# MLA's rotated queries with both terms on 128 rows, and low parts and sums of squares moved from GpSimd to VectorE

## The chip, the cores and the metric

The kernel runs on one core of a Trainium2 chip. TensorE does the matrix products and writes them into PSUM; VectorE, ScalarE and GpSimd do the elementwise work; SyncE (SP) issues most of the DMA transfers. The metric is the time on the device of one execution in microseconds (us), lower is better.

## The reference

The reference is a two-layer transformer block on 512 tokens of width 1024, in float32. Each layer has a mixer with four branches, and a gated feed-forward part; both are followed by a normalised residual sum. The branch that matters here is MLA, attention from latents, with 4 heads of 64 plain and 32 rotated dimensions:

```python
    q = heads(rms_norm(cq, mla_q_norm) @ w_uq, MLA_HEADS)
    kv = heads(rms_norm(ckv, mla_kv_norm) @ w_ukv, MLA_HEADS)
    k_rope = jnp.broadcast_to(rope(kr[:, None], pos), (B, MLA_HEADS, S, MLA_ROPE))
    q_mla = jnp.concatenate([q[..., :MLA_NOPE], rope(q[..., MLA_NOPE:], pos)], axis=-1)
    k_mla = jnp.concatenate([kv[..., :MLA_NOPE], k_rope], axis=-1)
    o_d = causal_block_attention(q_mla, k_mla, kv[..., MLA_NOPE:], (MLA_NOPE + MLA_ROPE) ** -0.5)
...
    x = x + rms_norm(mix, g_post_mix[l])
    h = rms_norm(x, g_pre_ffn[l])
    f = (jax.nn.silu(h @ w_ffn_gate[l]) * (h @ w_ffn_up[l])) @ w_ffn_down[l]
    x = x + rms_norm(f, g_post_ffn[l])
```

Rotation multiplies each rotated pair by a cosine and a sine and adds the two terms. `rms_norm` needs the sum of the squares of 1024 values for each token.

## The kernel before

All values lie transposed, features on the 128 partitions and the 512 tokens along the row. To reach float32 accuracy, every factor of a product is split into a high part (a rounded copy, made by ScalarE) and a low part (value minus high part, made by VectorE or GpSimd), and each product is made of three matmuls. `split_to` does this for activations (L483 high, L484 low; L486 and L487 with a scale). `conversion` does it for weights that a DMA brought (L297 high, L298 low).

The layer runs in this order: latents (a product with the weights of all branches' inputs), the four branches interleaved with each other, `out_block` (gates merged, output product, residual sum), the feed-forward part, and in layer 0 `down_block`, which already starts the latents of layer 1. `mla_prepare` is a generator that is advanced step by step between the other branches' products; work put off with `defer` runs one step later. It transposes the normalised latents, rotates the shared key (columns 128 to 192 of `ck`), transposes it (L867) to PSUM rows 64 to 96, and copies it to the keys of all four heads (`shared`). For each head it makes the query product (128 rows: 64 plain, 32 for the cosine and 32 for the sine term, arranged by the weights), and `q_out` scales, rotates and splits it to 96 rows. The values go through `v_split` (L928 to L933, half a PSUM bank each). Then the heads' scores (L634) are made, query block by query block, each by three matmuls; VectorE adds the mask and takes the row's maximum (L643), ScalarE takes the exponential (L645, with a load of its function table at the first), VectorE the reciprocal (L652), GpSimd scales (L653), and TensorE transposes the result (L660).

`square_sums` squares the eight column blocks of the new x on ScalarE (L1296) and adds four of them on GpSimd and four on VectorE (L1297), then both sums (L1035); TensorE sums over the partitions (L532, `token_sums`), and `rms_steps` and `root` make the factor: 1/sqrt with one correction (L516 to L524). `spread` (L562) brings the factor to all partitions by a matmul.

In `down_block` the new x, its normalised form and its high and low parts come by a generator (`renewal`, L1306 to L1312), half of the tokens at a time, while the latents' products of layer 1 (`latent_steps`, L1005 to L1007: high weight by high value, low weight by high value, high weight by low value) run in the order of the weight's eight row blocks. The table `at` says before which of these blocks a piece of the other work is put into the program. At `EA` = 2 the second half's factor chain, the rest of the renewal and two more weight conversions stand; there the low parts of four weight tiles of 128x452 are made.

Outside the parts under `ordered(True)` (there each engine follows the order of the code) a scheduler sets the order of instructions on each engine. SP issues its DMAs in one queue, in order: weights (L257), and moves of key halves from one SBUF tile to another (L1065, 64 rows of 512).

Of the kernel before, what the change touches and what calls it, by code (L numbers as in the profile page):

```python
# [9 lines left out]
F32 = mybir.dt.float32  # L10
# [7 lines left out]
S = 512  # L18
# [146 lines left out]
def constants():  # L165

    p = np.arange(128)[:, None]
    c = np.arange(128)[None, :]
    w = np.arange(512)[None, :]
    con = np.zeros((128, NCON), np.float32)  # L170

    def put(k, v):
        con[:, CON[k][0]:CON[k][1]] = v

    def rope(half):
        inv = np.float32(10000.0) ** (-np.arange(half, dtype=np.float32) / np.float32(half))
        ang = (np.arange(S, dtype=np.float32)[:, None] * inv[None, :].astype(np.float32)).astype(np.float64)
        cos = np.concatenate([np.cos(ang), np.cos(ang)], axis=1)
        sin = np.concatenate([-np.sin(ang), np.sin(ang)], axis=1)
        return cos, sin  # L180

    put("ident", p == c)
    put("tri", p <= c)
    put("blk", (p // 64 == c // 64) / 64.0)
    put("blk2", (p // 64 == np.arange(2)[None, :]) / 64.0)
    put("ones", 1.0)
    cos, sin = rope(16)
    put("tcos", cos.reshape(4, 128, 32).transpose(1, 0, 2).reshape(128, 128))
    put("tsin", sin.reshape(4, 128, 32).transpose(1, 0, 2).reshape(128, 128))
    s = 96.0 ** -0.5  # L190
    put("mrope", np.concatenate([np.zeros((64, S)), cos.T * s, sin.T * s]))
    d = 384 + p - w
    put("causal", np.where(d >= 0, 0.0, NEG))
    n = ((d >= 0) & (d <= 128)).astype(int) + ((d >= 0) & (d % 4 == 0)) + ((d >= 0) & (d % 16 == 0))
    put("dil", np.where(n > 0, np.log(np.maximum(n, 1)), NEG))
    cos, sin = rope(32)
    tab = np.zeros((6, 128, S), np.float32)
    tab[0] = np.concatenate([cos.T, cos.T])
    tab[1] = np.concatenate([sin.T, sin.T])
    for h in range(4):  # L200
        lg = np.log1p(-(2.0 ** (-5.0 - h)))
        tab[2 + h] = np.where(w >= p, np.exp(np.maximum(w - p, 0) * lg), 0.0)
    return {"con": con, "tab": tab}


class Builder:
# [622 lines left out]
    def mla_prepare(self, l, cq, ck, res):  # L829
        nc = self.nc  # L830
        ident = self.con("ident")
# [8 lines left out]
        for p in range(2):  # L840
            c = ck[p][:, 0:384].rearrange("p (t c) -> p t c", t=2)
            cs = slice(64 * p, 64 * p + 64)
            cos = self.con("tcos")[:, cs].rearrange("p (t c) -> p t c", t=2)
            sin = self.con("tsin")[:, cs].rearrange("p (t c) -> p t c", t=2)
            nc.vector.tensor_mul(c[:, :, 128:160], c[:, :, 128:160], cos)
            nc.vector.tensor_mul(c[:, :, 160:192], c[:, :, 160:192], sin)
            nc.vector.tensor_add(c[:, :, 128:160], c[:, :, 128:160], c[:, :, 160:192])
        yield
        cqT, ckT = [], []
        for kb in range(2):  # L850
            tp = self.ps("b")
            for t in range(4):
                o = 256 * (t % 2) + 128 * kb
# [3 lines left out]
        tp = self.ps("b")  # L857
        for t in range(4):
            o = 192 * (t % 2)
# [3 lines left out]
        K = [(self.ar(), self.ar()) for _ in range(4)]  # L863
        tp = self.ps("b")
        for t in range(4):
            o = 192 * (t % 2) + 64
            nc.tensor.transpose(tp[0:96, 128 * t:128 * t + 128], ck[t // 2][:, o:o + 96], ident)  # L867

        def shared(h):
            nc.scalar.copy(K[h][0][64:96, :], tp[64:96, :])  # L870
            if h == 0:
                nc.vector.tensor_sub(K[0][1][64:96, :], tp[64:96, :], K[0][0][64:96, :].bitcast(F32))
            else:
                nc.vector.tensor_copy(K[h][1][64:96, :], K[0][1][64:96, :].bitcast(F32))
        self.defer(lambda: [shared(h) for h in range(4)])
        yield
        rope = self.con("mrope")
        sc = 96.0 ** -0.5
        Q = []

        def q_out(ps):
            hi, lo = self.ar(), self.ar()
            self.split_to(hi[0:64, :], lo[0:64, :], ps[0:64, :], scale=sc)
            t1, t2 = self.a(), self.a()
            nc.vector.tensor_mul(t1[64:96, :], ps[64:96, :], rope[64:96, :])
            nc.vector.tensor_mul(t2[64:96, :], ps[96:128, :], rope[96:128, :])
            nc.vector.tensor_add(t1[64:96, :], t1[64:96, :], t2[64:96, :])
            self.split_to(hi[64:96, :], lo[64:96, :], t1[64:96, :], lo_engine=nc.gpsimd)
            Q.append((hi, lo))

        for h in range(4):
            ps = self.ps("b")
# [5 lines left out]
            ps = self.ps("b")  # L898
# [3 lines left out]
        for t in range(4):  # L902
            ts = slice(128 * t, 128 * t + 128)
            if t % 2 == 0:
                ps = self.ps("b")
            half = ps[:, 256 * (t % 2):256 * (t % 2) + 256]
            o = half.rearrange("p (h d) -> p h d", h=4)
# [7 lines left out]
                yield  # L915
        self.flush()
        for h in range(4):
            (q0, q1), (k0, k1) = ([t[0:96, :] for t in x[h]] for x in (Q, K))
            res["qk"].append(((q0, k0), (q0, k1), (q1, k0)))

    def v_split(self, src, scale=None):
# [107 lines left out]
    def square_sums(self):  # L1029

        acc = [None, None]
        for k in range(KT):
            i = k // 4
            acc[i] = self.add_square(acc[i], self.newx[k], (self.nc.gpsimd, self.nc.vector)[i])
        self.nc.vector.tensor_add(acc[0], acc[0], acc[1])  # L1035
        return acc[0]

# [326 lines left out]
    def down_block(self, xs, gain, x, next_gain):  # L1364


        nc = self.nc
        y, acc = self.columns("down", xs, gain, 7)
# [7 lines left out]
        ps, ss, r, rb, g, chain = {}, {}, {}, {}, {}, {}  # L1376
# [17 lines left out]
        def sums(half):  # L1394
            ss[half] = self.token_sums(acc, None, 2 * half, 2)
            r[half], chain[half] = self.rms_steps(ss[half], 2, self.eps[:, 2 * half:2 * half + 2])
# [8 lines left out]
        def some(g, n):  # L1405
            for _ in range(n):
                next(g, None)
# [4 lines left out]
        at = {i: [lambda: some(g[0], D0)] for i in range(DS + 1, FT)}  # L1412
        at[DA] = [lambda: sums(0), lambda: some(chain[0], 100)]
        at[DS] = [lambda: start(0)]
        lows = []

        def convert(engine=None):
            hi0, lo0, hi1, lo1 = self.conversion(engine)
            hi0()
            hi1()  # L1420
            lows.extend((lo0, lo1))
# [3 lines left out]
        squares(1)  # L1425
        lows.pop(0)()
        lows.pop(0)()
        at = {0: [lambda: some(g[0], 4), lambda: convert(nc.gpsimd)], 1: [lambda: some(g[0], 4)],
              EA: [lambda: sums(1), lambda: some(chain[1], 2), lambda: some(g[0], 4), lambda: some(chain[1], 2),
                   lambda: some(g[0], 4), lambda: some(chain[1], 100), lambda: some(g[0], 100),  # L1430
                   lambda: convert(nc.gpsimd), *(lambda: lows.pop(0)() for _ in range(4))],
              ES: [lambda: start(1), lambda: some(g[1], 4)]}
        wl = []
        for i in range(4):
# [417 lines left out]
def arrays_of(inputs):  # L1852
    r = lay_out({k: inputs[k] for k in _INS})
    r.update(constants())
    return r
# [15 lines left out]
```

## Time and profile before

| | |
|---|---|
| runs | 1717.69, 1714.25, 1713.33 us; median 1714.25 |
| profiled execution | 1716.04 us, span 1714.3 |
| mean granted clock of TensorE | 0.994 |
| PE (TensorE) busy | 1680.4 us, 98% |
| DVE (VectorE) busy | 1104.0 us, 64%, 2080 instructions |
| ACT (ScalarE) busy | 832.3 us, 49%, 1671 instructions |
| POOL (GpSimd) busy | 368.6 us, 21%, 368 instructions |

The span is the time from the first to the last instruction in the profile; the execution's own time has what lies around it as well. A busy share is a mean over stages. A granted clock of 1.00 is 2.4 GHz, 0.50 is 1.2 GHz.

### The profile page before, as it was taken

The page shows a single profiled execution, that of the slowest core. Times are in us where ns is not written, and L with a number is a line of the kernel's source. Part 1 is how long each engine was busy: PE and PEld are TensorE (multiplying, and loading weights), DVE is VectorE, ACT ScalarE, POOL GpSimd, SP SyncE. Part 2 cuts the span into 40 slices and gives each one's busy share as a digit, 9 for nine tenths or more (in the row PEclk, how much of TensorE's full clock was granted, in tenths as well). Part 3 has the DMA queues.
Part 4 walks back from the last instruction along what each step waited for, and adds up shares of the span by engine and source line. Part 5 has one row for each costly group of instructions (what it writes and reads, how often), then busy time and mean ns, then how long its engine had stood idle before and what let it go on. Part 6 is the DMA issues. An engine that isn't in the chain of part 4 may idle for free.

```text
span 1714.3 us, 27427 instructions
## 1 busy us (share of the span) xinstructions
PE 1680.4 (98%) x10340; PEld 1507.9 (88%) x10340; DVE 1104.0 (64%) x2080; ACT 832.3 (49%) x1671; POOL 368.6 (21%) x368
## 2 busy tenths in 40 slices
PE   9899999999999999999998999999999999999998
PEld 7788888888898999988877888878888989999998
DVE  6866767555468777752478577765454787777423
ACT  6566554323455555553356665532234555556422
POOL 1344333222131010000233353432222400000000
PEclk9999999999999999999999999999999999999999
DMA  5543325333434777343245343253334167773531
GB/s 188 155 117 111 96 90 154 99 92 94 159 115 122 184 185 181 91 156 102 66 134 149 100 129 86 87 160 94 103 92 160 51 184 181 188 184 81 166 90 59
DMA packets 74820, 215.90 MB, mean 126 GB/s; under 512 B 9536, under 2 KB 9792, under 8 KB 74688
## 3 DMA queue, kind: packets, MB, share of 16 engines
q1 hardware_dynamic: 69504, 195.28, 36.6%
q0 software_dynamic: 5184, 18.88, 6.7%
q8 instruction: 81, 1.33, 0.3%
q14 instruction: 51, 0.42, 0.1%
HBM read 189.47 MB, written 8.39 MB: 115 GB/s over the span
## 4 chain that ended last, share of the span: by engine, by line
PE 60%; DVE 5%; ACT 1%; issue 1%; POOL 1%; DMA 0%; DVEq 0%; SPq 0%; ACTq 0%; POOLq 0%
PE acc L491 8%; PE acc L492 8%; PE acc L493 8%; PE acc L465 4%; PE acc L467 4%; PE acc L466 4%; PE b L467 3%; PE b L466 3%; PE b L465 3%; PE b L983 1%; PE b L985 1%; PE b L984 1%; PE b L714 1%; DVE wlo L298 1%; PE b L634 1%
## 5 line engine op out<-in xcount | busy, mean ns | idle before, releaser
L491 PE MATMUL acc<-a,whi 128*128 128x512 f32 (+1 forms) x1238 | 478.3, 387 | 0.0
L493 PE MATMUL acc<-a,wlo 128*128 128x512 f32 (+1 forms) x1238 | 470.5, 380 | 0.0
L492 PE MATMUL acc<-a,whi 128*128 128x512 f32 (+1 forms) x1211 | 460.1, 380 | 0.0
L297 ACT CAST whi<-raw 128x512 fp32r<-128x512 f32 (+3 forms) x442 | 237.9, 579 | 389.4 <-issue 162.3
L298 DVE TENSOR_TENSOR wlo<-raw,whi 128x512 fp32r<-128x512 f32 (+3 forms) x438 | 302.3, 721 | 179.1 <-ACT whi L297 177.7
L493 PEld LDWEIGHTS acc<-a,wlo 128*128 128x128 f32 x1238 | 233.8, 189 | 44.1 <-issue 0.5
L491 PEld LDWEIGHTS acc<-a,whi 128*128 128x128 f32 x1238 | 234.5, 189 | 39.1 <-issue 1.0
L492 PEld LDWEIGHTS acc<-a,whi 128*128 128x128 f32 x1211 | 229.1, 189 | 39.0 <-DVE a L487 0.6
L465 PE MATMUL acc<-a,whi 128*128 128x256 f32 x560 | 158.6, 283 | 1.9 <-DVE a L1601 1.5
L466 PE MATMUL acc<-a,whi 128*128 128x256 f32 x560 | 158.4, 283 | 0.0
L467 PE MATMUL acc<-a,wlo 128*128 128x256 f32 x560 | 158.3, 283 | 0.0
L373 DVE TENSOR_TENSOR wlo<-raw,whi 128x1024 fp32r<-128x1024 f32 x90 | 110.3, 1225 | 57.1 <-ACT whi L372 53.8
L372 ACT CAST whi<-raw 128x1024 fp32r<-128x1024 f32 x90 | 94.5, 1050 | 95.2 <-PE acc L466 47.0
L1264 DVE TENSOR_TENSOR a<-acc,a 128x512 f32<-128x512 f32 x64 | 44.2, 691 | 137.1 <-PE acc L493 137.1
L465 PE MATMUL b<-a,whi 128*128 128x256 f32 x448 | 126.8, 283 | 0.0
L466 PE MATMUL b<-a,whi 128*128 128x256 f32 x448 | 126.8, 283 | 0.0
L467 PE MATMUL b<-a,wlo 128*128 128x256 f32 x448 | 126.8, 283 | 0.0
L1283 POOL TENSOR_TENSOR a<-a 128x512 f32<-128x512 f32 x48 | 70.5, 1469 | 237.8 <-DVE a L1282 229.1
L465 PEld LDWEIGHTS acc<-a,whi 128*128 128x128 f32 x560 | 107.4, 192 | 2.3 <-ACT whi L372 1.7
L484 POOL TENSOR_TENSOR a<-a 128x512 fp32r<-128x512 f32 (+1 forms) x48 | 67.0, 1395 | 191.4 <-ACT a L483 188.2
L466 PEld LDWEIGHTS acc<-a,whi 128*128 128x128 f32 x560 | 107.5, 192 | 0.1
L467 PEld LDWEIGHTS acc<-a,wlo 128*128 128x128 f32 x560 | 107.4, 192 | 0.0
(298 smaller groups left out, 3424.5 us busy)
## 6 DMA issues: line engine op xcount, KB each, us to landing
raw<-wts SPq DMA_DIRECT2D x260, 512.0 KB, 3.6
raw<-wts POOLq DMA_DIRECT2D x36, 512.0 KB, 6.1
a<-a SPq DMA_DIRECT2D x108, 128.0 KB, 2.3
raw<-wts SPq DMA_DIRECT2D x40, 256.0 KB, 2.6
a<-xT SPq DMA_DIRECT2D x16, 256.0 KB, 5.2
away<-a SPq DMA_DIRECT2D x16, 256.0 KB, 5.5
a<-away SPq DMA_DIRECT2D x16, 256.0 KB, 5.6
raw<-wts SPq DMA_DIRECT2D x7, 452.0 KB, 4.0
```

Source lines behind the costliest of these rows:

```text
L297: todo.append(lambda hi=hi, src=src, n=n: nc.scalar.copy(hi[:, :n], src))
L298: todo.append(lambda hi=hi, lo=lo, src=src, n=n: (lo_engine or nc.vector).tensor_sub(lo[:, :n], src, hi[:, :n].bitcast(F32)))
L372: nc.scalar.copy(hi, src)
L373: nc.vector.tensor_sub(lo, src, hi.bitcast(F32))
L465: mm(o, hi[:, c], x[k][0], start=first, stop=False, skip_group_check=i in (2, 3, 4, 6))
L466: mm(o, hi[:, c], x[k][1], start=False, stop=False, skip_group_check=i in (2, 3, 4, 6))
L467: mm(o, lo[:, c], x[k][0], start=False, stop=k == 3, skip_group_check=i in (2, 3, 4, 6))
L484: (lo_engine or nc.vector).tensor_sub(lo, src, hi.bitcast(F32))
L491: mm(out, w[0], x[0], start=start, stop=False)
L492: mm(out, w[0], x[1], start=False, stop=False)
L493: mm(out, w[1], x[0], start=False, stop=stop)
L1283: nc.gpsimd.tensor_add(merged[dd], merged[dd], t)
```

## The change

There are three parts. First, in `mla_prepare`, the rotated query is no longer summed: one multiplication by a constant (the scale on rows 0 to 64, scaled cosine and sine below) takes the product's 128 rows from PSUM, and a high and a low part of 128 rows are made. The shared key stands twice, on rows 64 to 96 and 96 to 128, so that the score product adds the two terms; its high and low part are made once, for head 0, and brought to heads 1 to 3 by six DMAs. Second, in `down_block`, the low parts of four latents' weight tiles are made on VectorE, not GpSimd. Third, `square_sums` makes all additions on VectorE.

```diff
-    put("mrope", np.concatenate([np.zeros((64, S)), cos.T * s, sin.T * s]))
+    put("mrope", np.concatenate([np.full((64, S), s), cos.T * s, sin.T * s]))
...
-            nc.vector.tensor_add(c[:, :, 128:160], c[:, :, 128:160], c[:, :, 160:192])
+            nc.vector.tensor_add(c[:, :, 160:192], c[:, :, 128:160], c[:, :, 160:192])
+            nc.vector.tensor_copy(c[:, :, 128:160], c[:, :, 160:192])
...
-            nc.tensor.transpose(tp[0:96, 128 * t:128 * t + 128], ck[t // 2][:, o:o + 96], ident)
-
-        def shared(h):
-            nc.scalar.copy(K[h][0][64:96, :], tp[64:96, :])
-            if h == 0:
-                nc.vector.tensor_sub(K[0][1][64:96, :], tp[64:96, :], K[0][0][64:96, :].bitcast(F32))
-            else:
-                nc.vector.tensor_copy(K[h][1][64:96, :], K[0][1][64:96, :].bitcast(F32))
-        self.defer(lambda: [shared(h) for h in range(4)])
-        yield
-        rope = self.con("mrope")
-        sc = 96.0 ** -0.5
+            nc.tensor.transpose(tp[:, 128 * t:128 * t + 128], ck[t // 2][:, o:o + 128], ident)
+
+        def shared():
+
+            hi, lo = (t[64:128, :] for t in K[0])
+            nc.scalar.copy(hi, tp[64:128, :])
+            nc.vector.tensor_sub(lo, tp[64:128, :], hi.bitcast(F32))
+            for h in range(1, 4):
+                for p in range(2):
+                    self.move(K[h][p][64:128, :], K[0][p][64:128, :])
+        self.defer(shared)
+        yield
         Q = []
 
         def q_out(ps):
-            hi, lo = self.ar(), self.ar()
-            self.split_to(hi[0:64, :], lo[0:64, :], ps[0:64, :], scale=sc)
-            t1, t2 = self.a(), self.a()
-            nc.vector.tensor_mul(t1[64:96, :], ps[64:96, :], rope[64:96, :])
-            nc.vector.tensor_mul(t2[64:96, :], ps[96:128, :], rope[96:128, :])
-            nc.vector.tensor_add(t1[64:96, :], t1[64:96, :], t2[64:96, :])
-            self.split_to(hi[64:96, :], lo[64:96, :], t1[64:96, :], lo_engine=nc.gpsimd)
-            Q.append((hi, lo))
+
+            f = self.a()
+            nc.vector.tensor_mul(f, ps, self.con("mrope"))
+            Q.append(self.split(f))
...
-            (q0, q1), (k0, k1) = ([t[0:96, :] for t in x[h]] for x in (Q, K))
+            (q0, q1), (k0, k1) = Q[h], K[h]
...
-            acc[i] = self.add_square(acc[i], self.newx[k], (self.nc.gpsimd, self.nc.vector)[i])
+            acc[i] = self.add_square(acc[i], self.newx[k], self.nc.vector)
...
-        at = {0: [lambda: some(g[0], 4), lambda: convert(nc.gpsimd)], 1: [lambda: some(g[0], 4)],
+        at = {0: [lambda: some(g[0], 4), lambda: convert()], 1: [lambda: some(g[0], 4)],
...
-                   lambda: convert(nc.gpsimd), *(lambda: lows.pop(0)() for _ in range(4))],
+                   lambda: convert(), *(lambda: lows.pop(0)() for _ in range(4))],
```


Below line 890 the lines of the changed kernel are three lower than before (L1060 is L1057, L933 is L930, L1297 is L1294); `shared`'s L872 is L874.

The order on VectorE in layer 0 behind the query products of heads 2 and 3 (`b_690` and `b_772`, in the changed kernel `b_682` and `b_759`; `wlo` is a weight's low part, `a_850`, then `a_832`, are values). Before:

```order
L487 SCALAR_TENSOR_TENSOR a_738<-b_690,a_737 64x512
L885 TENSOR_TENSOR a_741<-b_690,ct_79 32x512
L886 TENSOR_TENSOR a_742<-b_690,ct_79 32x512
L487 SCALAR_TENSOR_TENSOR a_792<-b_772,a_791 64x512
L887 TENSOR_TENSOR a_741<-a_741,a_742 32x512
L885 TENSOR_TENSOR a_795<-b_772,ct_79 32x512
L886 TENSOR_TENSOR a_796<-b_772,ct_79 32x512
L298 TENSOR_TENSOR wlo_918<-raw_714,whi_917 128x512
L887 TENSOR_TENSOR a_795<-a_795,a_796 32x512
L298 TENSOR_TENSOR wlo_918<-raw_714,whi_917 128x512
L298 TENSOR_TENSOR wlo_998<-raw_722,whi_997 128x512 x2
L933 TENSOR_TENSOR a_850<-b_820,a_850 128x4x64
```

In the changed kernel:

```order
L885 TENSOR_TENSOR a_729<-b_682,ct_79 128x512
L484 TENSOR_TENSOR a_732<-a_729,a_731 128x512
L885 TENSOR_TENSOR a_778<-b_759,ct_79 128x512
L298 TENSOR_TENSOR wlo_900<-raw_706,whi_899 128x512 x2
L484 TENSOR_TENSOR a_781<-a_778,a_780 128x512
L298 TENSOR_TENSOR wlo_980<-raw_714,whi_979 128x512 x2
L930 TENSOR_TENSOR a_832<-b_802,a_832 128x4x64
```

Eight operations on the two heads have become four, and they stand between the same conversions and the values' subtractions.

The order on VectorE in `down_block`, from the second half's root chain (L516 to L524) to the renewal that uses its factor. Before:

```order
L520 TENSOR_TENSOR sm2_8850<-sm2_8850,sm2_8848 128x2
L522 TENSOR_SCALAR sm2_8850<-sm2_8850 128x2
L524 TENSOR_TENSOR sm2_8849<-sm2_8849,sm2_8850 128x2
L1306 TENSOR_TENSOR a_8095<-a_8095,b_8888 128x256
L1306 TENSOR_TENSOR a_8100<-a_8100,b_8888 128x256
L1308 TENSOR_TENSOR a_8095<-a_8095,a_7907 128x256
L1306 TENSOR_TENSOR a_8204<-a_8204,b_8888 128x256
```

In the changed kernel:

```order
L520 TENSOR_TENSOR sm2_8832<-sm2_8832,sm2_8830 128x2
L522 TENSOR_SCALAR sm2_8832<-sm2_8832 128x2
L524 TENSOR_TENSOR sm2_8831<-sm2_8831,sm2_8832 128x2
L298 TENSOR_TENSOR wlo_8808<-raw_8585,whi_8807 128x452 x2
L298 TENSOR_TENSOR wlo_8845<-raw_8705,whi_8844 128x452 x2
L1303 TENSOR_TENSOR a_8077<-a_8077,b_8870 128x256
L1303 TENSOR_TENSOR a_8082<-a_8082,b_8870 128x256
L1305 TENSOR_TENSOR a_8077<-a_8077,a_7889 128x256
L1303 TENSOR_TENSOR a_8186<-a_8186,b_8870 128x256
```

The four low parts, GpSimd's before, stand between the end of the chain and the renewal.

The order on VectorE for the sums of squares of layer 0's mixer output, the renewal's last step ahead of it. Before:

```order
L1297 TENSOR_TENSOR a_5249<-a_5249,a_5251 128x512
L1297 TENSOR_TENSOR a_5249<-a_5249,a_5254 128x512
L1297 TENSOR_TENSOR a_5249<-a_5249,a_5257 128x512
L1035 TENSOR_TENSOR a_5238<-a_5238,a_5249 128x512
L298 TENSOR_TENSOR wlo_5300<-raw_5024,whi_5299 128x512 x2
```

In the changed kernel:

```order
L1294 TENSOR_TENSOR a_5220<-a_5220,a_5222 128x512
L1294 TENSOR_TENSOR a_5220<-a_5220,a_5225 128x512
L1294 TENSOR_TENSOR a_5220<-a_5220,a_5228 128x512
L1294 TENSOR_TENSOR a_5231<-a_5231,a_5233 128x512
L1294 TENSOR_TENSOR a_5231<-a_5231,a_5236 128x512
L1294 TENSOR_TENSOR a_5231<-a_5231,a_5239 128x512
L1032 TENSOR_TENSOR a_5220<-a_5220,a_5231 128x512
L298 TENSOR_TENSOR wlo_5282<-raw_5006,whi_5281 128x512 x2
```

The three additions of the first half stand ahead of those of the second.

## Rows read from the trace of the kernel before

**Rows 1.** What TensorE waited for: released by, us in all, times, longest us.
```profile
PE b L634 <- DVE a L933: 4.4, 2, 3.0
PE b L660 <- POOL a L653: 3.9, 5, 1.8
...
PE b L562 <- DVE sm L524: 2.8, 1, 2.8
...
PE b L532 <- DVE a L1035: 1.8, 2, 0.9
...
PE b L493 <- DVE wlo L298: 0.6, 1, 0.6
```

**Rows 2.** Windows: busy us (instructions) of PE, PEld, DVE, ACT, POOL; PEclk; DMA; GB/s.
```profile
85.30:92.10 6.80, 6.03 (x15) 4.97 (x16) 3.40 (x11) 5.59 (x14) 1.81 (x2) 0.50 0.33 96
860.10:863.50 3.40, 3.40 (x11) 3.13 (x12) 2.23 (x6) 1.02 (x2) 1.40 (x2) 0.51 0.56 163
942.10:945.50 3.40, 3.40 (x11) 2.73 (x10) 1.78 (x9) 2.28 (x7) 2.03 (x3) 0.50 0.17 39
```

**Rows 3.** Groups by line and shape: busy us, mean ns, idle before them.
```profile
L634 PE MATMUL b<-a 128*128 128x512 f32 x32 | 10.2, 400 | 0.1
...
L634 PE MATMUL b<-a 96*128 96x512 f32 x24 | 7.5, 424 | 0.0
...
L484 DVE TENSOR_TENSOR a<-a 128x512 fp32r<-128x512 f32 x54 | 35.3, 686 | 4.9 <-ACT a L483 4.7
...
L885 DVE TENSOR_TENSOR a<-b,ct 32x512 f32<-32x512 f32 x8 | 5.5, 689 | 0.2
...
L484 POOL TENSOR_TENSOR a<-a 32x512 fp32r<-32x512 f32 x8 | 11.0, 1374 | 18.7 <-ACT a L483 18.4
```

**Rows 4.** Timeline, layer 0: start us, us, instructions; in brackets idle time and releaser.
```profile
80.76 3.93 DVE L298 TENSOR_TENSOR wlo<-raw,whi 128x512 fp32r<-128x512 f32 x3
...
84.72 0.42 DVE L933 TENSOR_TENSOR a<-b,a 128x256 fp32r<-128x256 f32 x1
...
86.07 1.33 PE L634 MATMUL b<-a 96*128 96x384 f32 x3 [3.00 <-DVE a L933]
```

**Rows 5.** Timeline of ScalarE, layer 1, before the first softmax.
```profile
938.78 1.28 ACT L645 ACT_TABLE_LOAD   x1
940.07 0.40 ACT L645 ACTIVATE a<-a,sm 128x128 f32<-128x128 f32 x1
```

**Rows 6.** Timeline, layer 0: SP's queue and ScalarE's next conversions.
```profile
63.26 14.23 SPq L1065 DMA_DIRECT2D a<-a  x12
...
81.91 8.84 SPq L257 DMA_DIRECT2D raw<-wts  x3
...
98.26 1.14 ACT L297 CAST whi<-raw 128x512 fp32r<-128x512 f32 x2 [0.45 <-PE acc L492]
```

**Rows 7.** DMA issues (part 6 of the page): count, KB each, us to landing.
```profile
raw<-wts SPq DMA_DIRECT2D x260, 512.0 KB, 3.6
```

**Rows 8.** Timeline around the latents' weights in down_block, and of the steps before.
```profile
844.54 0.16 DVE L524 TENSOR_TENSOR sm<-sm,sm 128x2 f32<-128x2 f32 x1
...
849.82 0.63 DVE L1312 SCALAR_TENSOR_TENSOR a<-a,vt 128x256 fp32r<-128x256 f32 x1
...
854.57 5.01 POOL L298 TENSOR_TENSOR wlo<-raw,whi 128x452 fp32r<-128x452 f32 x4
...
854.88 2.61 DVE L1312 SCALAR_TENSOR_TENSOR a<-a,vt 128x256 fp32r<-128x256 f32 x2
...
857.61 0.90 DVE L518 TENSOR_TENSOR sm<-sm 128x2 f32<-128x2 f32 x1
...
860.05 1.17 PE L562 MATMUL b<-ct,sm 128*128 128x128 f32 x4 [2.79 <-DVE sm L524]
```

**Rows 9.** Timeline of the sums of squares, layer 0, end of the mixer.
```profile
512.71 4.39 POOL L1297 TENSOR_TENSOR a<-a 128x512 f32<-128x512 f32 x3 [1.67 <-ACT a L1296]
...
514.75 3.70 DVE L1297 TENSOR_TENSOR a<-a 128x512 f32<-128x512 f32 x3 [2.63 <-ACT a L1296]
```

## Prediction

> **What bounds the kernel now.** I read the share of the engines first (the table above): TensorE is busy nearly the whole span, VectorE two thirds of it, the rest less. So only two things can give time back: gaps in TensorE, and stretches in which its clock is granted at half. The list of what TensorE waited for comes next [rows 1]. The reader is to see that all of its longer waits but the first one of the program end on VectorE or, once, GpSimd, and that four of the listed lines lie just where the change works: the scores of the MLA heads (L634, 4.4 us in two waits), the factors' spread in the last block of layer 0 (L562, 2.8), the sums of squares (L532, 1.8 in two) and a low part of a weight (L493, 0.6). The fifth (L660) is the first transpose behind those scores. Then the windows [rows 2]: after three of these waits the granted clock is 0.50 or 0.51, that is 1.2 GHz, for 6.8, 3.4 and 3.4 us, in stretches where TensorE is nearly always busy; at 2.4 GHz the same work would take half, so they cost 3.4, 1.7 and 1.7 us beside the waits themselves. Everything else in the list is outside the change.
>
> **The change, part by part.**
>
> *MLA queries and keys, prices.* A VectorE operation of 512 columns costs 0.69 us whether it has 128 rows or 32 [rows 3]. Per head, four of these (L487, L885, L886, L887: 2.75 us) become two (1.38), and one GpSimd subtraction of 1.37 us and one of two ScalarE operations go. The longer product is free: with 128 rows a score matmul of 512 columns averages 400 ns, with 96 it averages 424 [rows 3]. The two small copies in the preparation (64 columns each) cost a few tenths in a stretch where TensorE has other products; I charge nothing, and at most 0.4 us per layer if that cover fails.
>
> *MLA, layer 0.* TensorE stops for 3.00 us before the third score group, from 83.07 (86.07 less 3.00), because the PSUM bank is held by the values' L933 [rows 4]. That L933 started at 84.72, right behind three conversions L298 that took 3.93 us together while GpSimd ran: 1.31 each, where such an operation alone takes 0.69. In the new order the last two heads put 2 × 1.37 = 2.7 us less in front of it, and with no L484 left on GpSimd the three L298 fall towards 2.1, another 1.9. So L933 (now L930) starts near 80.1, and the bank, which was free 1.35 us after its start, is free near 81.5: before 83.07. The wait goes, with 1.6 us to spare; since the scheduler has redrawn TensorE's order here too, I leave 0.4 of it. What is late next is the first softmax: the mask's addition, the load of the exponential table, the exponential, the reciprocal and GpSimd's scaling, which TensorE's transposes L660 wait for. In layer 0 the half clock hid this chain (TensorE's other work took twice as long); without it I take 1.0 us of wait there, and 0.4 at the next transposes. Layer 0: 3.0 + 3.4 − 0.4 − 1.0 − 0.4 = 4.6 us; bounds 2.6 (half clock again for half of its time, longer waits) and 6.4.
>
> *MLA, layer 1.* Here TensorE waits 1.4 us for L933 (4.4 less the 3.0 of layer 0) and 1.8 us at L660, the longest of its five [rows 1], and from 942.1 it runs at half clock [rows 2]. With VectorE relieved by the same 4.6 us the first wait goes. The second is the chain behind the table load: load 1.28 us [rows 5], exponential, then scaling. It begins earlier by what the scores begin earlier, but TensorE also arrives earlier; I leave 0.8 of the 1.8, and no half clock, since TensorE has then waited a quarter of what it did before. 1.4 + 1.0 + 1.7 = 4.1 us; bounds 2.4 (the half clock comes all the same) and 4.9.
>
> The table load is where a rule speaks against this. In the row it starts at 938.78 and the exponential starts at 940.07, 0.01 us after its end: 1.28 us and nothing more [rows 5]. The Trainium skill (ScalarE: Activation LUTs, "What ACT_TABLE_LOAD costs") gives about 2.66 us for every switch of tables, the load and a drain of about 1.38. By that page, as an estimate, the wait at L660 would be 1.4 us longer in each layer and the sum 2.8 us smaller; the rows show no drain, and I go by them.
>
> *SP's queue.* The keys of heads 1 to 3 no longer come from six ScalarE and VectorE copies but from six DMAs of 128 KB, in front of the twelve key moves that stand there now. Those twelve take 14.23 us, 1.19 each [rows 6], so six put 7.1 us in front at most. The weight loads behind them, from 81.91 on, would go out from 89 on at the latest, and land 3.6 us later in the median [rows 7], near 93; ScalarE's next conversions of weights behind this stage begin at 98.26 [rows 6]. That is 5 us of slack: I charge nothing, and with the cover gone it would cost each us beyond the slack, in both layers.
>
> *Low parts in down_block.* TensorE waits 2.79 us for L524, the last step of a reciprocal root, until 860.05 [rows 1, 8]. Ahead of it on VectorE stand two L1312 that took 2.61 us and tiny steps such as L518 with 0.90, both while GpSimd made four low parts in 5.01 us. Without GpSimd such an L1312 takes 0.63 and such a step 0.16 (0.2 with its spacing, an estimate) [rows 8]. So 854.88 + 1.26 + 5 × 0.2 gives L524 done near 857.1, 2.9 earlier. But the four low parts now stand behind it on VectorE, and TensorE needs two of them in products that stand ahead of L562: 2 × 0.6 (from 0.69 for 512 columns) and one product more, so L562 starts near 858.5. Gain 1.55; a wait of about 1 us appears at the products, where GpSimd's low part came in time before. The half clock that followed the 2.79 [rows 2] goes if a wait split in two does not bring it: I take that, 1.7. The L493 wait of 0.6, which stands behind sums of squares that are earlier now, goes too. 3.8 us; bounds 1.5 and 5.1.
>
> *Sums of squares.* Before each L532 VectorE idles 2.63 us for the second half's squares, then makes three additions in 3.70 us beside GpSimd's three (4.39) [rows 9]. The additions that come from GpSimd fit into that idle time, and all go at 0.69 once GpSimd is quiet. They began at 514.75 and the last sum stood behind them; with the three first ones done by then and three at 0.69, a little held by the squares still to come, it is done near 517.3 rather than 519.2. TensorE wins only what it waited: 1.8 us in the two layers [rows 1]. VectorE's steps behind it wait for TensorE, so nothing more comes. In the first block TensorE does not wait for these sums: 0. If VectorE were full there, the moved work would cost 1.9 us a place.
>
> Sum: 4.6 + 4.1 + 3.8 + 1.8 = 14.3 us. The profiled execution took 1716.04, which gives 1701.7; the median of the runs is 1.8 lower, which gives 1700.0. I put **1701.0**.
>
> **The rivals.**
> - *The waits form again at the softmax chain, and the half clock with them.* For it: L660 already ends such a chain, and 1.8 us of wait was followed by half clock [rows 1, 2]. Against: the chain starts earlier by as much as the scores. About 1 us more at L660 and 1.7 of half clock, in each layer: 5.4 back, 1706.4. The drain that the Trainium skill gives (ScalarE: Activation LUTs, "What ACT_TABLE_LOAD costs") would work the same way; by it, as an estimate, 2.8 us would come back if the clock holds, 1703.8.
> - *All of the waits go*, as GpSimd's absence frees ScalarE's chain as well: 6.4 + 4.9 + 5.1 + 1.8 = 18.2, 1697.
> - *It does not do what it says*: the bank waits for ScalarE's casts (L932, behind weight conversions) rather than VectorE, and the low parts behind L524 give back what L524 gains. Then only the sums of squares and L493 are left, some 2.4 us: 1712.5. Against it: rows 4 show L933 right behind the L298.
> - *Slower, by SP's queue.* If the six moves held the queue longer than the slack, weights would land late and TensorE would stand. To end 0.3% above before, 14.3 + 5.1 us must be lost, 9.7 per layer beyond 5 of slack: 7.6 us more queue than the 7.1, so over twice 1.19 for each move. Time 1720. Rows 6 speak against it, unless a move waits there for its source and holds the others.
>
> **How the numbers follow.** A measurement of this kernel tells about 0.3% (5 us) from no change. Forecast 0.55 (1698 to 1704.5), waits again 0.17, all gone 0.12, nothing 0.11, slower 0.05. Forecast, waits again and all gone are faster by over 5 us: 0.84, with 0.02 of the third's better end 0.86 in all. Same 0.10, slower 0.04 (its milder end lies within 0.3%). From 1696 to 1709 lies the forecast with most of its two neighbours, some 8 in 10.
>
> **What would show it.** Right: no wait at the third scores of layer 0 and half clock neither at 85 nor at 860; L298 beside them at 0.69; L660 with 0.5 to 1.2 us; a new wait of about 1 us at the latents' low products; none at L532. Wrong: half clock still at 85 or 942, a wait on a weight DMA behind 90, or L930 no earlier than 84.

## The result and the profile after

The changed kernel takes 1703.62 us in the median (1702.81 to 1705.07, 4 runs) against 1713.85 (1713.33 to 1717.69, 4 runs): 10.2 us less by the medians; the ratio is 0.9937, 95% interval 0.9924 to 0.995, which is some 10.8 us less. Forecast were 1701.0, in a range of 1696 to 1709.

The first part of the page of the changed kernel (span, then busy us of each engine):

```profile
span 1703.3 us, 27371 instructions
PE 1674.1 (98%) x10340; PEld 1503.2 (88%) x10340; DVE 1086.8 (64%) x2078; ACT 823.0 (48%) x1657; POOL 335.6 (20%) x344
```

The span falls by 11.0 us. TensorE's busy time falls from 1680.4 (the table above) to 1674.1, by 6.3, with the same matmuls: that is stretches at half clock that are gone (by the windows here and in [rows 2], 17.0 us of them before and 3.4 after, and half of the difference is 6.8). The rest of the span, when TensorE stands, falls from 33.9 to 29.2, by 4.7. So between these two profiles more than half of the gain came through the clock, and the waits gave less than their list of before promised. But the profile of the kernel before was one at the low end: its mean granted clock was 0.994, where seven other runs of that kernel (the comparison of e8 below) had 0.994 to 0.998, 0.9954 in the mean, and four of the changed kernel there 0.998. Taken as (1 − clock) × span, an estimate, these are 7.8 and 3.4 us lost, so over the runs some 4 of 12 us came through the clock. What TensorE waited for in the changed kernel:

```profile
PE b L660 <- POOL a L653: 4.7, 6, 1.8
PE b L868 <- DVE a L1057: 3.5, 2, 1.9
...
PE b L491 <- DVE a L487: 2.8, 2, 1.4
...
PE acc L1003 <- DVE wlo L298: 1.4, 1, 1.4
...
PE b L493 <- DVE wlo L298: 0.3, 1, 0.3
```

Against [rows 1]: the scores (L634, 4.4), the spread (L562, 2.8) and the sums of squares behind L1035 (1.8) no longer appear at all. New is the low product L1003 with 1.4. L660 has grown from 3.9 to 4.7, and L491 stands at 2.8. Two rows of the kernel before that the prediction had no use for are needed beside these, from the same list:

```profile
PE b L867 <- DVE a L1060: 3.1, 2, 2.0
...
PE b L491 <- DVE a L487: 0.6, 1, 0.6
```

So L491 has gained 2.2 us and the key's transposes (L867, now L868) 0.4. Windows of the changed kernel at the places of [rows 2] (the second one behind L562, the third behind L868 of layer 1):

```profile
85.30:92.10 6.80, 5.67 (x30) 4.61 (x30) 3.81 (x16) 6.26 (x16) 4.57 (x6) 1.00 0.04 10
854.10:857.50 3.40, 3.40 (x20) 3.17 (x19) 3.19 (x8) 1.40 (x3) 1.96 (x3) 1.00 0.83 261
896.30:899.70 3.40, 2.92 (x23) 2.72 (x23) 1.97 (x2) 2.97 (x6) 1.30 (x1) 1.00 0.39 131
933.40:936.90 3.50, 3.50 (x12) 2.80 (x11) 2.06 (x11) 1.92 (x6) 2.21 (x4) 0.51 0.32 74
```

The window of the kernel before that answers to the third, behind L867 of layer 1:

```profile
904.50:907.90 3.40, 3.40 (x19) 3.39 (x18) 2.87 (x4) 3.40 (x7) 1.28 (x1) 0.50 0.49 145
```

The clock is 1.00 in three of the four places; it is 0.51 only behind the first transposes of layer 1. The kernel before also had a fourth stretch at half clock, at 904.5, which I had left out of the account; in the changed kernel the same wait is not followed by one.

The timeline of the three stages, changed kernel (layer 0's scores, layer 1's first softmax, `down_block`, sums of squares):

```profile
80.64 1.28 DVE L298 TENSOR_TENSOR wlo<-raw,whi 128x512 fp32r<-128x512 f32 x2
...
82.44 0.42 DVE L930 TENSOR_TENSOR a<-b,a 128x256 fp32r<-128x256 f32 x1 [0.52 <-ACT a L929]
...
88.75 0.33 PE L660 MATMUL b<-ct,a 128*128 128x128 f32 x1 [1.13 <-POOL a L653]
...
928.28 0.42 DVE L930 TENSOR_TENSOR a<-b,a 128x256 fp32r<-128x256 f32 x1
...
929.39 0.41 ACT L929 CAST a<-a 128x256 fp32r<-128x256 f32 x1
...
929.82 1.28 ACT L645 ACT_TABLE_LOAD   x1
...
931.11 0.40 ACT L645 ACTIVATE a<-a,sm 128x128 f32<-128x128 f32 x1
...
932.33 0.33 PE L660 MATMUL b<-ct,a 128*128 128x128 f32 x1 [1.82 <-POOL a L653]
...
852.18 0.16 DVE L524 TENSOR_TENSOR sm<-sm,sm 128x2 f32<-128x2 f32 x1
...
852.25 2.24 DVE L298 TENSOR_TENSOR wlo<-raw,whi 128x452 fp32r<-128x452 f32 x4
...
852.93 0.47 PE L1003 MATMUL acc<-wlo,a 128*128 128x452 f32 x1 [1.35 <-DVE wlo L298]
...
854.07 0.61 PE L562 MATMUL b<-ct,sm 128*128 128x128 f32 x4
...
509.53 4.48 DVE L1294 TENSOR_TENSOR a<-a 128x512 f32<-128x512 f32 x6 [0.54 <-ACT a L1293]
...
514.05 0.69 DVE L1032 TENSOR_TENSOR a<-a 128x512 f32<-128x512 f32 x1
```

L298 beside the queries takes 0.64 in place of 1.31 [rows 4]; the values' L930 starts at 82.44 rather than 84.72, and the scores behind it no longer wait. But the first transposes do, 1.13 us in layer 0 and 1.82 in layer 1: in layer 1 the last of the values' subtractions (928.28) and, on ScalarE, the scalings and casts of another branch's values (until 929.80), then the table load (1.28), exponential and scaling, stand one behind the other until L660 at 932.33. In `down_block` the root chain's last step starts at 852.18, and the four low parts behind it take 2.24; the first low product waits for the first of them, 1.35 us, and L562 behind it for nothing. In the sums of squares, the six additions take 4.48 us one after the other, and the last sum ends at 514.74, ahead of the matmuls that need it.

### The profile page after: what moved, and what is told of

Read it like the earlier page. It is cut to its first block, busy times and chain, and to the rows that moved or that the text cites. A ratio compares the mean times of both kernels' runs of the same rounds, so it can differ in the third digit from the quotient of the medians.

```text
span 1703.3 us, 27371 instructions
## 1 busy us (share of the span) xinstructions
PE 1674.1 (98%) x10340; PEld 1503.2 (88%) x10340; DVE 1086.8 (64%) x2078; ACT 823.0 (48%) x1657; POOL 335.6 (20%) x344
## 4 chain that ended last, share of the span: by engine, by line
PE 61%; DVE 4%; ACT 1%; issue 1%; DMA 1%; POOL 0%; DVEq 0%; ACTq 0%
PE acc L491 8%; PE acc L492 8%; PE acc L493 8%; PE acc L465 4%; PE acc L467 4%; PE acc L466 4%; PE b L467 3%; PE b L466 3%; PE b L465 3%; PE b L980 1%; PE b L982 1%; PE b L981 1%; PE b L714 1%; DVE wlo L298 1%; PE b L634 1%
## 5 line engine op out<-in xcount | busy, mean ns | idle before, releaser
L491 PE MATMUL acc<-a,whi 128*128 128x512 f32 (+1 forms) x1238 | 478.0, 386 | 0.0
L493 PE MATMUL acc<-a,wlo 128*128 128x512 f32 (+1 forms) x1238 | 469.4, 379 | 0.0
L297 ACT CAST whi<-raw 128x512 fp32r<-128x512 f32 (+3 forms) x442 | 237.5, 577 | 392.4 <-issue 162.1
L298 DVE TENSOR_TENSOR wlo<-raw,whi 128x512 fp32r<-128x512 f32 (+3 forms) x442 | 301.2, 713 | 183.2 <-ACT whi L297 182.1
L493 PEld LDWEIGHTS acc<-a,wlo 128*128 128x128 f32 x1238 | 233.3, 188 | 44.1 <-issue 0.5
L491 PEld LDWEIGHTS acc<-a,whi 128*128 128x128 f32 x1238 | 234.0, 189 | 38.7 <-issue 1.0
L465 PE MATMUL acc<-a,whi 128*128 128x256 f32 x560 | 158.5, 283 | 1.9 <-DVE a L1598 1.5
L465 PE MATMUL b<-a,whi 128*128 128x256 f32 x448 | 126.8, 283 | 0.0
L465 PEld LDWEIGHTS acc<-a,whi 128*128 128x128 f32 x560 | 107.4, 192 | 2.3 <-ACT whi L372 1.7
L335 POOL DMA_DIRECT2D raw<-wts x36 | 31.2, 868 | 354.8 <-DMA raw<-wts 195.6
```

What stands on the lines that cost most here:

```text
L297: todo.append(lambda hi=hi, src=src, n=n: nc.scalar.copy(hi[:, :n], src))
L298: todo.append(lambda hi=hi, lo=lo, src=src, n=n: (lo_engine or nc.vector).tensor_sub(lo[:, :n], src, hi[:, :n].bitcast(F32)))
L465: mm(o, hi[:, c], x[k][0], start=first, stop=False, skip_group_check=i in (2, 3, 4, 6))
L491: mm(out, w[0], x[0], start=start, stop=False)
L493: mm(out, w[1], x[0], start=False, stop=stop)
```

## The experiments

**The three parts alone** (e1, e2, e3) undo the other two. e1 is the changed kernel with

```diff
-            acc[i] = self.add_square(acc[i], self.newx[k], self.nc.vector)
+            acc[i] = self.add_square(acc[i], self.newx[k], (self.nc.gpsimd, self.nc.vector)[i])
...
-        at = {0: [lambda: some(g[0], 4), lambda: convert()], 1: [lambda: some(g[0], 4)],
+        at = {0: [lambda: some(g[0], 4), lambda: convert(nc.gpsimd)], 1: [lambda: some(g[0], 4)],
...
-                   lambda: convert(), *(lambda: lows.pop(0)() for _ in range(4))],
+                   lambda: convert(nc.gpsimd), *(lambda: lows.pop(0)() for _ in range(4))],
```

> Only the part in the MLA preparation (queries and keys on 128 rows), on the kernel before; the low parts of the latents' weights and the first half's additions stay on GpSimd. Theory (the three parts act each in its own place and add up): 5.2 us below the kernel before, the two shifts that the trace of the changed kernel shows over the MLA stages (3.1 in layer 0, 2.1 in layer 1); waits at L634 gone in both layers, new waits of about 1.4 at L491 behind L487, L562 still 2.8 with half clock behind it. Rival (the gain comes through the half clock of other places): under 3 us, or over 7.

e2 is the kernel before with `convert()` in the two places, e3 the kernel before with the one line of `square_sums`.

> Only the low parts of the latents' weights in down_block on VectorE, on the kernel before. Theory: L562's wait of 2.8 us gives way to one of 1.3 to 1.4 us at the low products in front of it, and the half clock behind it goes: 3.1 us below before. Rival (a wait split in two still brings the half clock): 1.4 below before, PEclk 0.5 near 860 as before. MLA stages as before: L634 waits 3.0 and 1.4.

> Only the sums of squares on VectorE, on the kernel before. Theory: the two L532 waits of 0.9 and the L493 wait of 0.6 go, 2.4 us below before, and the first block is unchanged. Rival (VectorE is full behind the sums, so the added work comes back at the feed-forward part's first waits, L1601 and L1610): 0 to 1 below before, those waits 1 us longer.

Measured against the kernel before on the same chip: e1 0.9972 (0.9961 to 0.9984), 4.8 us less; e2 0.9983 (0.9973 to 0.9992), 2.9 less; e3 0.9979 (0.9968 to 0.999), 3.6 less. Together 11.3, against 10.8 for the change as a whole: the parts add up, as closely as their intervals (some 2 us to either side of each) can tell. What TensorE waited for in e1:

```profile
PE b L660 <- POOL a L653: 4.3, 6, 1.8
...
PE b L562 <- DVE sm L524: 2.8, 1, 2.8
```

In e2:

```profile
PE b L634 <- DVE a L933: 4.4, 2, 3.0
...
PE b L493 <- DVE wlo L298: 1.7, 1, 1.7
...
PE acc L1006 <- DVE wlo L298: 1.3, 1, 1.3
```

In e3:

```profile
PE b L634 <- DVE a L933: 4.4, 2, 3.0
...
PE b L660 <- POOL a L653: 3.4, 6, 1.8
...
PE b L562 <- DVE sm L524: 2.8, 1, 2.8
```

Each part removes its own waits (in e1 the two at L634 are gone, in e3 those at L532) and leaves the waits of the other two parts at L634, L562 and L532 at their size to a tenth. L660 (3.2 us in e2, 3.9 before) and the key's transposes (2.3 in e2, 3.1 before) move by up to 0.8 us although no edit of e2 or e3 touches them. In e2 the L562 wait turned into 1.3 at the low product as expected, but the L493 wait behind the sums of squares grew from 0.6 to 1.7: a part of what the low parts gain is given back there as long as the sums are late. In the change as a whole, where the sums are early, it is 0.3.

What was not expected is the clock. A window of e1, behind a wait of 0.88 us at L532:

```profile
1363.00:1366.40 3.40, 3.40 (x17) 3.40 (x18) 2.41 (x10) 1.23 (x3) 0.00 (x0) 0.50 0.46 154
```

A window of e3, behind the 2.80 us at L562:

```profile
860.30:863.70 3.40, 3.40 (x19) 3.16 (x20) 2.72 (x7) 1.33 (x3) 1.89 (x3) 1.00 0.57 183
```

A wait of 0.88 us is followed by half clock, and one of 2.80 is not, though in the kernel before it was [rows 2]. It is not always as long either: behind the 3.0 us at L634 it lasted 6.8 us in the kernel before and in e3, and 3.4 in e2 and e10. Over the twelve profiles taken (before, changed, ten experiments):

| wait | us | followed by half clock |
|---|---|---|
| L634, layer 0 | 3.0 | 4 of 4 |
| L562 | 2.8 | 3 of 4 |
| L660, layer 1 | 1.8 | 5 of 6 |
| L867 or L868, layer 1 | 1.2 to 2.3 | 4 of 12 |
| L867 or L868, layer 0 | 0.8 to 2.1 | 2 of 12 |
| L532 behind L1035 | 0.9 | 1 of 8 |
| L493, where it is over 0.5 (before, e2, e7, e10) | 0.6 to 1.7 | 1 of 4 (0.9 in e7) |
| low product in front of L562 (L1003 in the changed kernel) | 1.35 | 0 of 7 |
| L465, first products of the feed-forward part | 1.5 to 1.6 | 0 of 12 |

The waits of 0.5 to 1.6 us at L491 and the shorter ones at L634 and L660 were followed by none.

The longest waits bring it most often, but no length decides it: 2.33 us at L868 was not followed by one, 0.88 was, and the 1.5 at L465 never was.

**The table load** (e4): the changed kernel with one line behind the loop over the heads in `mla_prepare`:

```diff
+        self.defer(lambda: nc.scalar.activation(self.small(1), Q[1][1][:, 0:1].bitcast(F32), AF.Exp))
         for t in range(4):
```

> The changed kernel with one exponential of one column on ScalarE behind the second head's query (a small extra operation), so that the table of the exponential is loaded some 10 us before the first softmax. Theory (the wait at L660 that is left is the table load in the softmax chain): L660's waits of 1.1 and 1.8 us shrink by 1 us or more each and the half clock near 933 goes, 3 to 4 us below the changed kernel, 13 to 14 below before. Rival (the chain is set by the values' casts ahead of it on ScalarE and by the mask's addition behind the values on VectorE): L660 waits shrink by under 0.4 us, time within 1.5 us of the changed kernel.

Measured: 1700.81 us, ratio 0.9913 (0.9897 to 0.993), 14.9 us below before. Against the changed kernel that is some 4 us by its 0.9937 above and 2.4 by its 0.9927 in the comparison of e8, and the intervals overlap both times: in time, unclear. Timeline of layer 1, ScalarE and TensorE:

```profile
912.91 1.28 ACT L899 ACT_TABLE_LOAD   x1
...
914.21 0.20 ACT L899 ACTIVATE sm<-a 128x1 f32<-128x1 f32 x1
...
928.07 0.40 ACT L645 ACTIVATE a<-a,sm 128x128 f32<-128x128 f32 x1
...
929.38 0.33 PE L660 MATMUL b<-ct,a 128*128 128x128 f32 x1 [0.52 <-POOL a L653]
```

The load ends 14 us ahead of the first exponential, where ScalarE has time, and L660 waits 0.52 rather than 1.82; in layer 0 it does not wait. The difference of 1.30 is the load's 1.28 alone. So the load was worth its full length in the wait that was left. The other branch's casts still stand in that chain (the exponential starts at 928.07, behind a cast begun at 927.75); what moving them would give was not tried. The half clock behind L660 was gone here, but one came behind L868.

**Contention or count** (e5): `q_out` with `Q.append(self.split(f, lo_engine=nc.gpsimd))`.

> The changed kernel with the low parts of the queries (L484, 128x512, one per head) back on GpSimd, so VectorE has one operation per head fewer than in the changed kernel and GpSimd is busy beside it again. Theory (half of the gain in the MLA stages came from GpSimd's silence, since VectorE's subtractions took 1.31 us beside it and 0.69 without): L298 beside them near 1.3 us again, the values' L930 2 us later or more, a wait of 1 us or more at the third scores of layer 0 and 1.5 to 4 us above the changed kernel. Rival (the number of VectorE's operations decides): no wait at the scores, time within 1 us of the changed kernel.

Measured: 1702.07 us, 0.9926 (0.9908 to 0.9943), against 0.9927 (0.9912 to 0.9942) for the changed kernel in the same comparison. Timeline of layer 0 in e5:

```profile
77.48 3.71 DVE L298 TENSOR_TENSOR wlo<-raw,whi 128x512 fp32r<-128x512 f32 x3 [0.35 <-ACT whi L297]
...
82.44 0.80 PE L634 MATMUL b<-a 128*128 128x384 f32 x3 [1.10 <-DVE a L930]
...
87.47 0.33 PE L660 MATMUL b<-ct,a 128*128 128x128 f32 x1 [0.51 <-POOL a L653]
```

The list of its waits:

```profile
PE b L660 <- POOL a L653: 3.0, 6, 1.1
PE b L634 <- DVE a L930: 2.0, 2, 1.1
```

The mechanism is as the theory had it: L298 takes 1.24 us again and the third scores wait 1.10. But the time is the same, and the theory falls in its price. L634 waits 1.10 more in layer 0 and 0.94 in layer 1; L660 behind it waits less, 0.51 for 1.13 and 1.06 for 1.82. So two thirds of the wait at the scores (1.4 of 2.0 us) are paid out of the wait at the softmax behind them. The other 0.7 us do not show in the time, which the intervals would hide; this profile also had no stretch at half clock where the changed kernel's had one (1.7 us).

**The key moves** (e6): in `shared`, for heads 1 to 3, copies in place of the six DMAs.

```diff
-                for p in range(2):
-                    self.move(K[h][p][64:128, :], K[0][p][64:128, :])
+                nc.scalar.copy(K[h][0][64:128, :], tp[64:128, :])
+                nc.vector.tensor_copy(K[h][1][64:128, :], lo.bitcast(F32))
```

> The changed kernel with the keys of heads 1 to 3 copied by ScalarE (high parts) and VectorE (low parts), three each of 64x512 per layer, in place of the six DMAs. Theory (the six DMAs are hidden in SP's slack, and so would be the copies): time within 1.5 us of the changed kernel, the waits at L491 of 1.4 us unchanged. Rival (the moves hold up weights on SP): those waits fall to 0.6, no wait on weights elsewhere, 1.5 us or more below the changed kernel.

Measured: 1700.54 us, 0.9912 (0.9897 to 0.9927), 2.4 us under the changed kernel's median in the same comparison, with intervals that overlap: unclear. The waits at L491 did not fall (1.6 and 0.8 us), so the rival's mechanism is not what made it faster; L660 waited 0.7 at layer 1 rather than 1.8. In part that goes with a redrawn order: two weight casts (L297), which in the changed kernel stand among the values' casts on ScalarE (925.75 and 926.81), come behind the first exponential in e6, and from the first cast of values out of PSUM to the table load there are 4.13 us in place of 4.61. So e6 does not price the moves alone. The profile had no stretch at half clock either. In SP's queue the moves cost little, as forecast: 18 transfers from 60.34 on in the changed kernel, then the next weight, by SP's timeline:

```profile
60.34 18.70 SPq L1062 DMA_DIRECT2D a<-a  x18
...
79.39 2.89 SPq L257 DMA_DIRECT2D raw<-wts  x2
```

SP's timeline in e6, with 12 transfers from 63.85 on:

```profile
63.85 12.56 SPq L1062 DMA_DIRECT2D a<-a  x12
...
78.64 2.09 SPq L257 DMA_DIRECT2D raw<-wts  x2
```

The weight goes out 0.75 us later.

**Low parts first** (e7): e4, with two of the four low parts inside the root chain.

```diff
-                   lambda: some(g[0], 4), lambda: some(chain[1], 100), lambda: some(g[0], 100),
-                   lambda: convert(), *(lambda: lows.pop(0)() for _ in range(4))],
+                   lambda: some(g[0], 4), lambda: lows.pop(0)(), lambda: lows.pop(0)(),
+                   lambda: some(chain[1], 100), lambda: some(g[0], 100),
+                   lambda: convert(), *(lambda: lows.pop(0)() for _ in range(2))],
```

> The kernel with the early table load, and in down_block two of the four low parts between the second and third step of the root chain instead of behind it. Theory (the wait of 1.35 us at the low product is the first low part's place behind the chain): that wait falls to 0.7 to 0.9, L562 waits at most 0.3, time 0.5 us below the early table alone: 13 to 14 below before. Rival: the chain is held up by as much as the low parts come earlier, L562 waits 0.8 or more, no gain.

Measured: 1700.98 us, 0.9915 (0.9897 to 0.9932), like e4. The list of waits in e7:

```profile
PE b L493 <- DVE wlo L298: 0.9, 1, 0.9
...
PE acc L1004 <- DVE wlo L298: 0.8, 1, 0.8
```

The low product waits 0.8 rather than 1.35 and L562 does not wait, as expected; but L493 waits 0.9 rather than 0.3. The 0.6 us came back 17 us later, as in e2, and here the 0.9 at L493 was followed by 3.4 us at half clock.

**The changed kernel again** (e8), without an edit.

> The changed kernel once more, unchanged. Theory (whether a wait is followed by half clock changes from execution to execution, while the waits stay): the same waits within 0.3 us (L660 1.1 and 1.8, low product 1.35, L868 1.9, L491 1.4 in both layers), but half clock at another of these places or at none; time 10 us below before. Rival (the place of the half clock belongs to the program): half clock behind the L660 wait of layer 1 again, and there alone.

Measured: 1702.95 us, 0.9927 (0.9912 to 0.9942). The list of waits in this profile:

```profile
PE b L660 <- POOL a L653: 4.3, 6, 1.8
...
PE b L491 <- DVE a L487: 1.7, 2, 1.1
...
PE acc L1003 <- DVE wlo L298: 1.4, 1, 1.4
```

L660 (1.8 again, with half clock behind it again) and the low product are the same to a few hundredths; so in this the rival was right. L868 of layer 1 is not (1.19 for 1.94), and L491 is not: 0.56 and 1.09 us in the two layers, for 1.42 and 1.38 in the first profile of the same program. Ahead of it in layer 0, ScalarE's cast waits for a weight's transfer. In the first profile, then in this one:

```profile
54.35 0.62 ACT L297 CAST whi<-raw 128x512 fp32r<-128x512 f32 x1 [1.69 <-DMA raw<-wts]
```

```profile
51.80 0.62 ACT L297 CAST whi<-raw 128x512 fp32r<-128x512 f32 x1 [0.66 <-DMA raw<-wts]
```

These casts start 6.5 and 5.7 us after SP's first issue of these weights. What TensorE waits at L491 goes with what ScalarE waits here: where this is 1.5 to 1.9 us (the first profile, e1, e4, e5, e6), L491 waits 1.2 to 1.6, and where it is 0.5 to 0.9 (before, e2, e3, e7, e8), L491 waits 0.6. (In e9 and e10 a stretch at half clock lies in between, and L491 does not wait.)

**Both, and the kernel before with the early load** (e9: e4 and e6 together; e10: e4's line in the kernel before, on 64 rows).

> The changed kernel with both the early table load and the keys of heads 1 to 3 copied by ScalarE and VectorE instead of moved by DMAs. Theory (both act on the same wait, the first transposes' L660, so they don't add): no wait over 0.5 us at L660 in the MLA stages, 13 to 15.5 us below before, as with either alone. Rival (they add up): 16 us or more below before.

> The kernel before, with only the exponential of one column behind the second head's query, so that its table is loaded early. Theory (in the kernel before, two chains stand one behind the other, the values' subtractions and then the softmax; shortening the second alone takes the wait at L660 of layer 1 and nothing else): L634 waits 3.0 and 1.4 us stay, the L660 wait of 1.8 falls under 0.8, 1 to 3 us below before. Rival (the wait at the scores decides and the rest is hidden behind it): within 1 us of before.

Measured: e9 1699.51 us, 0.9907 (0.9892 to 0.9923), 16.0 below before, the lowest of all; with e4 at 0.9913 and e6 at 0.9912 it can't be said whether they add. e10: 0.9995 (0.9985 to 1.0004), no change. The list of waits in e10:

```profile
PE b L634 <- DVE a L934: 4.4, 2, 3.0
...
PE b L660 <- POOL a L653: 2.4, 6, 0.6
```

L634 keeps its 4.4 us, and L660 falls from 1.8 at most to 0.6, as the theory had it for the waits. The price, 0.9 us by the ratio (2.6 less to 0.7 more by the interval) for 1.5 us less wait at L660, fits the rival and leaves only the low end of the theory's 1 to 3 us.

## Why the prediction was right, and where its sizes were off

*What bounds the kernel* held: each of the four places gave up its wait when its own part was made, and outside them what moved by more than a few tenths were the waits at L491, at L493 (e2), at the key's transposes and at L660, and the clock.

*MLA, layer 0* (4.6 forecast). The wait of 3.0 at L634 went, with the 6.8 us at half clock behind it (3.4 us), and a wait of 1.13 us appeared at L660, where 1.0 was forecast; the 0.4 us left at the scores and the 0.4 at the next transposes did not come. By these terms 5.3, of which the 3.4 was the full 6.8 us at half clock of one profile; the same wait brought 3.4 us of it in e2 and e10. The step on contention was right in what it named (L298 0.64 for 1.31, L930 earlier), but L930 came at 82.44, not 80.1: VectorE now waits for ScalarE's casts, which I had not followed. And e5 shows no time for contention by itself, within its interval.

*MLA, layer 1* (4.1 forecast). This is the term that was mis-sized. The 1.4 at L634 went. But of the 1.8 at L660 I left 0.8, and no half clock; all 1.8 stayed, and the half clock behind it too (1.7). "It begins earlier by what the scores begin earlier, but TensorE also arrives earlier" was the right sentence, and it says that nothing is gained; I took 1.0 for it all the same. e4 shows what it takes: the load out of the chain. Here 1.4 us of the 4.1 came; 1.7 came besides, from the half clock behind L867 that did not return, and that was chance (4 of 12). The prediction's own signs say the same: half clock behind this wait was one of its signs of being wrong, and 1.82 lies above the 0.5 to 1.2 that it gave L660.

*The table load.* Here the Trainium skill (ScalarE: Activation LUTs, "What ACT_TABLE_LOAD costs") would have about 2.66 us for each switch. The traces don't agree: in the changed kernel the exponential starts at 931.11, 0.01 us after the load's 1.28, and taking the load out of the chain took 1.30 off the wait.

*A cost charged at nothing.* L491 waits 2.2 us more than before. I had named no cover for it, since [rows 1] hardly show it. In layer 0 the wait goes with the landing of a weight, and differs by 0.9 us between two executions of the same program. Of the profiles without half clock just ahead of it, five of seven with the MLA part have the long wait there and none of three without it, so the change may have a share; how much is open. In layer 1 the stretch at half clock, which in the kernel before made TensorE arrive later, had hidden it: in all four profiles with such a stretch behind L867 or L868 (before, e4, e7, e9) L491 does not wait there, and in the eight without it waits 0.4 to 1.4.

*SP's queue* held: nothing waits for a weight behind the moves.

*Low parts* (3.8 forecast): L562 2.8 gone, 1.35 in its place (forecast: a wait of about 1 and a gain of 1.55; measured 1.45), half clock gone, L493 down by 0.3 rather than 0.6. 1.45 + 1.7 + 0.3 = 3.4. Alone it measured 2.9; the 0.3 at L493 belongs to the sums of squares, since e3 alone has it and e2 alone has 1.1 more. The clock term is no certain gain, by the table: 3 of 4 such waits of 2.8 bring it, and 1.35 in its place never did.

*Sums of squares* (1.8 forecast): both waits went, 1.8; alone it measured 3.6, where the waits at L532 (1.8) and L493 (0.6 to 0.3) explain 2.1. The rest lies within the interval (1.7 to 5.5 us), and the clock agrees with it: 0.9966 in the mean of e3's eleven runs, for 0.9956 in 22 of the kernel before, an estimated 1.6 us.

*The sum.* Between the two profiles these terms give 5.3 + 3.1 + 3.4 + 1.8, less 2.2 at L491 and 0.4 at the key's transposes: 11.0, as the spans differ, with smaller waits left out. Against the 14.3 forecast that is 0.7 more in layer 0, 1.0 less in layer 1, 0.4 less at the low parts, and 2.6 of waits that were charged at nothing. The clock's terms (3.4 + 1.7 + 1.7 = 6.8) were taken from one profile with a clock of 0.994; over all runs the clock gave back some 4 us. That the median came out only 2.6 us from the forecast is in part luck: of the 2.7 us that layer 1 lacked at L660, the stretch behind L867 made 1.7 good.

Of the rivals, "the waits form again at the softmax chain" is what happened in layer 1, and half of its price came.

Still open: whether e4 and e6 are faster than the changed kernel in time, and the change's own share in the wait at L491. The extra copies on VectorE in the preparation were not tried by themselves.

## What to carry to other kernels

Before a wait is booked as gain, look at what stands behind it: where two chains end close together (here the values' subtractions and the first softmax), shortening the first pays only the distance to the second, and the second is found by asking what TensorE meets next and who releases it. A table load in such a chain is moved out by one small operation with the same function, early, where it holds up nothing; here that took 1.30 us off the wait, and what it gave in time is not clear of the noise. And a half clock behind a wait is a chance to be weighted by how often it comes, not a fixed price.

## What the runs showed of the hardware

Whether a stop of TensorE is followed by 3.4 us (or 6.8) at 1.2 GHz changes from kernel to kernel at the same stop: it came behind 0.88 us (e1, L532) and did not behind 2.80 (e3, L562), a stop that it followed in three other profiles. Between the two profiles of the change, busy time of TensorE fell by 6.3 us through this, more than all the waits gave (4.7); over all runs it was about a third of the gain, an estimate from the mean clocks. And the same program's transfers of weights in layer 0 were cast 5.7 and 6.5 us after their issue in two executions, ScalarE waiting 0.66 and 1.69 us for them, and a wait of TensorE behind them differed by 0.9 us.
